# The closing Silu of each scan group, written as two ACT operations

## The chip, the cores and the metric

The kernel runs on one core of a Trainium2 chip. The metric is device time in microseconds (us) of one execution, 1267.39 us as the median of three runs (1267.34 to 1268.09). Times inside the kernel are read from one profiled execution, counted from the start of its span.

## What is computed

Two residual layers over 512 tokens of width 1024, each followed by a SwiGLU feed-forward part. Layer 0 mixes tokens in two ways at once: neighbourhood attention in 8 heads, and a bidirectional state-space scan (SSD) in 4 groups of 4 heads. The change sits in the scan's inputs:

```python
xbc = jax.nn.silu(centred_depthwise_conv(xbc, conv_w, conv_b))
xs, bm, cm = jnp.split(xbc, [...])
...
def gated_group_rms_norm(y, z, g):
    h = (y * jax.nn.silu(z)).astype(jnp.float32).reshape(Bsz, S, SSD_GROUPS, Dn // SSD_GROUPS)
    h = h * lax.rsqrt(jnp.mean(h * h, axis=-1, keepdims=True) + NORM_EPS)
    return (h.reshape(Bsz, S, Dn) * g.astype(jnp.float32)).astype(y.dtype)
```

So Silu is applied to x, B and C after a convolution of four taps, and to the gate z without one. The scan then takes exponentials of running sums; the norms take a reciprocal square root, made here as a logarithm (Ln), an exponential (Exp of -0.5 times it) and one Newton step.

## The kernel before, in words

Activations are kept transposed, 128 features by 512 tokens to a tile. Every product in full precision is three TensorE (PE) passes over two-part operands (`mm3`, lines 165 to 167); `load_w` (lines 145 to 161) fetches a weight tile by DMA, copies its high part on ScalarE (ACT, line 152, out `w_h` or `wo_h`, `wq_h`, `wf_h`) and subtracts on VectorE (DVE, line 154, out `w_l` and so on).

`even_mixer` is layer 0's mixer. Its PE work is one long stream, `fill`, of weight blocks of 24 matmuls (8 steps of 3), into which the attention's and the scan's own matmuls are put: `run(n)` takes n steps of `fill`. The blocks are query and key projections, then for each scan group g six blocks (`ssd_blocks`), then the output projection (`out_blocks`, PSUM tiles `oA` for what is ready early and `oB` for the last two groups, which are groups 2 and 3).

A group's six results make one tile `grp` (`gt` in the code) of 128 x 6 x 512. The blocks come in the order 4, 5, 0, 1, 2, 3. Parts 4 and 5 are z: a plain copy out of PSUM on ACT (line 546). Parts 0 to 3 are B, C and two tiles of x: `conv` makes one ACT operation (line 530) and three DVE operations (line 533) of each. After part 3 one Silu runs over the whole tile (line 550), and `preload_act_table_set(LNEXP)` (line 553) makes ACT load the table set that holds both Exp and Ln. `issue_after` puts that load behind the Silu, `high_priority` puts it there as early as may be. A load of a table set is an ACT instruction, ACT_TABLE_LOAD. Those that the code does not write are put by the compiler in front of an activation whose function is not in the set that is then loaded; for an Ln or an Exp alone it picks sets that do not hold the other one.

`ssd_group` scans a group: PE transposes B and x (`bt`, `xt`, lines 568 and 575), makes C times B (`cb`, line 581) and chunk states (`st`, line 604). For each half i of the heads (two heads, hh 0 and 1) ACT and DVE make the decay weights: ACT copies with scales (`m` line 640, `mb` 642), adds (`cf`, 643), takes an Exp (`cf<-cf`, line 650); DVE takes minima and multiplies (lines 645, 647, 649, 651). The product of line 651 is what PE's `yd` (line 656) needs, followed by `yo` (669) and DVE's sums into y (660 to 674). `ssd_norm` then makes the group's norm: squares (`gsq`, 686), `gs` on PE (693, 694), then on ACT `gn_m` (204), Ln (214), Exp (215), Square (216), Newton on DVE (208, 209), `yn` (698), and the two parts `so_xh` on ACT (188), `so_xl` on DVE (189), which the output projection reads. The norm's second piece is started NORM_LAG steps (12, 14, 10, 8) after its first; SSD_QUOTA gives the steps of `fill` between the pieces of a scan, LEAD (15, 12, 14, 8) those between a group's last block and its scan.

The feed-forward part of layer 0 begins with the same chain on one tile `fr` (`norm` in `ffn`, lines 1070 to 1073), whose result scales everything after it up to the hidden tiles (`hh`, `hl`), which the first matmuls of the down projection (`fo`) read.

The order of work: inside the scans PE's instructions stay as the program is written (`manual_schedule`); ACT, DVE, POOL and the DMA queue (SP) are ordered by a scheduler that takes what is ready by its own estimate, in the priority of program order. An instruction that becomes ready early may therefore be issued ahead of older ones. In the feed-forward part PE, DVE and ACT all stay as written. On the chip every engine runs its list strictly in order. Table loads that the compiler adds are put in after that ordering.

Of the kernel before, what the change touches and what calls it, by code (L numbers as in the profile page):

```python
# [11 lines left out]
AF = mybir.ActivationFunctionType  # L12
# [65 lines left out]
def encoder_kernel(ctx: ExitStack, tc: tile.TileContext, xt, vec, cst, rope, nab, w_v, w_qk, w_dt, w_ssd,  # L78
                   w_o0, w_t0, w_fa, w_fb, w_kv, w_gv, w_gq, w_o1, out):
    nc = tc.nc  # L80
    V, A, G, T = nc.vector, nc.scalar, nc.gpsimd, nc.tensor
# [13 lines left out]
    def bank(name, tag="p"):  # L95
        if tag in turns:
            turns[tag].append(turns[tag].pop(0))
            tag = turns[tag][-1]
        return pp.tile([P, S], F32, name=name, tag=f"p{tag}", bufs=BANKS[tag])
# [44 lines left out]
    def load_w(src, cols, name, eng=None, los=None):  # L144
        hi = wsp.tile([P, 1024], F32R, name=f"{name}_h", tag="wh", bufs=WH)
        lo = wsp.tile([P, 1024], F32R, name=f"{name}_l", tag="wl", bufs=WL)
        raw = wsp.tile([P, 1024], F32, name=f"{name}_r", tag="wr", bufs=WR)[:, 0:cols]
        parts = src if isinstance(src, list) else [src]
        for n, part in enumerate(parts):
            w = cols // len(parts)  # L150
            nc.sync.dma_start(raw[:, n * w:(n + 1) * w], part)
        A.activation(hi[:, 0:cols], raw, AF.Copy)  # L152
        def low():
            (eng or V).tensor_tensor(lo[:, 0:cols], raw, f(hi)[:, 0:cols], ALU.subtract)  # L154

        if los is None:
            low()
        else:
            los.append(low)
        return hi, lo  # L160

    def mm3(ps, w, wc, x, xc, first, last, wn=P, skip=False):
        (wh, wl), (xh, xl) = w, x
        a, b = slice(wc, wc + wn), xc
        T.matmul(ps, wl[:, a], xh[:, b], start=first, stop=False, skip_group_check=skip)  # L165
        T.matmul(ps, wh[:, a], xl[:, b], start=False, stop=False, skip_group_check=skip)  # L166
        T.matmul(ps, wh[:, a], xh[:, b], start=False, stop=last, skip_group_check=skip)  # L167
# [65 lines left out]
    def even_mixer(lp):  # L233
# [295 lines left out]
        def conv(ps, cb, o):  # L529
            A.activation(o, ps, AF.Identity, scale=vc("conv_w", cb * 4 + 2), bias=vc("conv_b", cb))  # L530
            for j in (0, 1, 3):
                a, b = max(0, 2 - j), min(S, S + 2 - j)
                V.scalar_tensor_tensor(o[:, a:b], ps[:, a + j - 2:b + j - 2], vc("conv_w", cb * 4 + j), o[:, a:b],
                                       ALU.mult, ALU.add)

        def ssd_blocks(g):
            gt = lp.tile([P, 6, S], F32, name=f"grp{g}", tag="grp", bufs=3)
            conv_cols = (8 + g, 12 + g, 2 * g, 2 * g + 1)

            def matmuls(w, i):  # L540
                ps = bank(f"g{g}_{i}")
                for k in range(KB):
                    mm3(ps, w, k * P, xn[k], ALL, k == 0, k == KB - 1)
                    yield
                if i > 3:
                    A.activation(gt[:, i], ps, AF.Copy)  # L546
                else:
                    conv(ps, conv_cols[i], gt[:, i])
                if i == 3:
                    si = A.activation(gt, gt, AF.Silu)  # L550
                    with tc.issue_after(si.ins):
                        with tc.high_priority():
                            A.preload_act_table_set(LNEXP)
                    ready[g] = gt

            for i in (4, 5, 0, 1, 2, 3):
                yield (lambda i=i: load_w(w_ssd[g * 6 + i], 1024, f"w{g}_{i}", V)), lambda w, i=i: matmuls(w, i)
# [1008 lines left out]
```

## Time and profile before

| | |
|---|---|
| median of 3 runs | 1267.39 us (1267.34 to 1268.09) |
| profiled execution, its own time | 1266.3 us |
| its span | 1264.5 us |
| granted TensorE clock, mean | 1.00 |
| the four scans and the end of layer 0's mixer | about 158 to 357 us |
| start of the feed-forward part of layer 0 | about 357 us |

A profile row of the timeline reads: start in us, duration in us, engine, line, operation, out<-in, shapes, number merged, and in brackets the idle time before it with what ended it. Neighbouring ACT operations overlap by about a tenth of a us, so a start-to-start distance is a little less than a duration. Rows of waits read: who waited, for whom, us in total, how often, longest.

### The profile page before, as it was taken

What the parts mean: (1) busy time and instruction counts of PE and PEld (TensorE: products, weight loads), DVE (VectorE), ACT (ScalarE), POOL (GpSimd) and SP (SyncE); (2) the same over time, 40 slices, a digit from 0 to 9 for tenths busy, and PEclk for the clock granted to TensorE, in tenths of its full rate; (3) what the DMA queues carried; (4) which work ended last, traced back from release to release, by engine and by line L of the source; (5) the groups of instructions that cost most, each with busy time, mean ns of one, the idle gap of its engine ahead of it and who ended that gap; (6) DMA issues with size and microseconds to landing.
All of it is one profiled execution on the core that took longest, in us unless ns stands there. A gap on an engine that the chain in (4) does not pass through costs nothing.

```text
span 1264.5 us, 20138 instructions
## 1 busy us (share of the span) xinstructions
PE 1252.1 (99%) x7574; PEld 1098.4 (87%) x7574; DVE 991.4 (78%) x1637; ACT 730.3 (58%) x1384; POOL 117.6 (9%) x161
## 2 busy tenths in 40 slices
PE   9999999999999999999999999999999999999998
PEld 8778788888788999989998888788888999889987
DVE  6788798999779988739854879998779988558732
ACT  6676578778464565415643558787554556336521
POOL 5022010011000000000000013444000000000000
PEclk9999999999999999999999999999999999999999
DMA  7335353556243333323223452321242333423132
GB/s 239 109 104 156 112 142 117 166 146 198 79 148 98 104 114 101 117 84 101 78 80 111 133 125 82 95 51 34 71 126 89 116 102 101 117 83 101 55 119 93
DMA packets 54241, 139.03 MB, mean 110 GB/s; under 512 B 7232, under 2 KB 9664, under 8 KB 54144
## 3 DMA queue, kind: packets, MB, share of 16 engines
q1 hardware_dynamic: 53712, 137.13, 35.8%
q8 instruction: 59, 0.97, 0.3%
q10 hardware_dynamic: 432, 0.63, 0.2%
q14 instruction: 38, 0.31, 0.1%
HBM read 127.11 MB, written 2.23 MB: 102 GB/s over the span
## 4 chain that ended last, share of the span: by engine, by line
PE 95%; ACT 2%; DVE 2%; issue 0%; DMA 0%; DVEq 0%; ACTq 0%
PE fo L166 6%; PE fo L167 6%; PE fo L165 6%; PE fa L167 5%; PE fa L166 5%; PE fa L165 5%; PE fu L1029 3%; PE fg L1029 3%; PE g L165 3%; PE g L166 3%; PE g L167 3%; PE fb L167 3%; PE fb L166 3%; PE fb L165 3%; PE opt L1311 2%; PE vps L286 2%
## 5 line engine op out<-in xcount | busy, mean ns | idle before, releaser
L165 PE MATMUL fo<-hh,wf_l 128*128 128x512 f32 x352 | 137.0, 389 | 0.0
L166 PE MATMUL fo<-hl,wf_h 128*128 128x512 f32 x352 | 137.0, 389 | 0.0
L167 PE MATMUL fo<-hh,wf_h 128*128 128x512 f32 x352 | 136.9, 389 | 0.0
L152 ACT ACTIVATE wf_h<-wf_r 128x1024 fp32r<-128x1024 f32 (+1 forms) x72 | 65.5, 913 | 119.2 <-PE fo L167 71.6
L1002 DVE TENSOR_TENSOR xr<-xr,fo 128x512 f32<-128x512 f32 (+1 forms) x49 | 32.1, 673 | 108.8 <-PE fo L167 108.8
L1302 POOL TENSOR_SCALAR op<-op,osum 128x512 f32<-128x512 f32 x64 | 45.6, 726 | 491.2 <-DMA QS<-qa_sh 433.5
L154 DVE TENSOR_TENSOR wf_l<-wf_r,wf_h 128x1024 fp32r<-128x1024 f32 (+1 forms) x72 | 74.0, 1044 | 11.0 <-ACT wf_h L152 11.0
L165 PEld LDWEIGHTS fo<-hh,wf_l 128*128 128x128 f32 x352 | 66.1, 188 | 13.7
L166 PEld LDWEIGHTS fo<-hl,wf_h 128*128 128x128 f32 x352 | 66.1, 188 | 13.7
L167 PEld LDWEIGHTS fo<-hh,wf_h 128*128 128x128 f32 x352 | 66.1, 188 | 13.6
L165 PE MATMUL g<-n_xh,w_l 128*128 128x512 f32 x192 | 76.9, 401 | 0.8 <-ACT grp L546 0.8
L166 PE MATMUL g<-n_xl,w_h 128*128 128x512 f32 x192 | 75.3, 392 | 0.5 <-DVE n_xl L189 0.5
L167 PE MATMUL g<-n_xh,w_h 128*128 128x512 f32 x192 | 75.3, 392 | 0.0
L926 ACT ACTIVATE sl<-sb 128x256 f32<-128x256 f32 x36 | 15.1, 419 | 96.1 <-DVE sb L925 96.1
L1298 ACT ACTIVATE op<-os,omx 128x512 f32<-128x512 f32 x64 | 43.8, 686 | 17.3 <-DVE omx L1296 13.5
L807 ACT ACTIVATE sa<-fa 128x256 f32<-128x256 f32 x72 | 26.9, 374 | 38.1 <-PE fa L167 38.1
L1296 DVE TENSOR_REDUCE omx<-os 128x1 f32<-128x512 f32 x64 | 42.5, 680 | 6.6 <-PE os L1294 6.5
L1315 DVE TENSOR_TENSOR opt<-opt,opt 128x512 fp32r<-128x512 f32 x64 | 43.3, 682 | 4.1 <-ACT opt L1314 3.3
L1314 ACT ACTIVATE opt<-opt 128x512 fp32r<-128x512 f32 x64 | 38.0, 596 | 14.0 <-PE opt L1311 13.3
L810 DVE TENSOR_TENSOR gl<-gr,gh 128x1024 fp32r<-128x1024 f32 x36 | 43.8, 1218 | 0.0
L165 PEld LDWEIGHTS g<-n_xh,w_l 128*128 128x128 f32 x192 | 36.1, 188 | 8.3 <-ACT grp L546 1.2
L807 ACT ACTIVATE gh<-gr 128x1024 fp32r<-128x1024 f32 x36 | 37.7, 1048 | 9.4 <-PE fo L167 9.4
(2745 smaller groups left out, 4305.4 us busy)
## 6 DMA issues: line engine op xcount, KB each, us to landing
ur<-in_w_fa SPq DMA_DIRECT2D x36, 512.0 KB, 3.6
gr<-in_w_fa SPq DMA_DIRECT2D x36, 512.0 KB, 3.6
w_r<-in_w_ssd SPq DMA_DIRECT2D x24, 512.0 KB, 3.6
wf_r<-in_w_fb SPq DMA_DIRECT2D x32, 320.0 KB, 3.0
wf_r<-in_w_fa SPq DMA_DIRECT2D x16, 512.0 KB, 3.6
wf_r<-in_w_fb SPq DMA_DIRECT2D x16, 512.0 KB, 3.5
nb<-in_nab SPq DMA_DIRECT2D x16, 256.0 KB, 3.2
ec<-ecumd SPq DMA_DIRECT2D x32, 128.0 KB, 3.0
```

The source lines that it names most:

```text
L152: A.activation(hi[:, 0:cols], raw, AF.Copy)
L154: (eng or V).tensor_tensor(lo[:, 0:cols], raw, f(hi)[:, 0:cols], ALU.subtract)
L165: T.matmul(ps, wl[:, a], xh[:, b], start=first, stop=False, skip_group_check=skip)
L166: T.matmul(ps, wh[:, a], xl[:, b], start=False, stop=False, skip_group_check=skip)
L167: T.matmul(ps, wh[:, a], xh[:, b], start=False, stop=last, skip_group_check=skip)
L807: A.activation(dst, src, AF.Copy, scale=scale)
L810: V.tensor_tensor(lo, t, f(hi), ALU.subtract)
L1029: T.matmul(ps, (wl if p == 0 else wh)[:, k * P:k * P + P], xl if p == 1 else xh, start=m == 0, stop=m == 23)
L1296: V.tensor_reduce(mx, sps, AX.X, ALU.max, negate=True)
L1298: A.activation(p_, sps, AF.Exp, bias=mx, accum_out=sums)
L1302: G.tensor_scalar(p_, p_, sums, 1.0, ALU.mult, ALU.mult)
L1315: V.tensor_tensor(hl[:, S:2 * S], pt, f(hl[:, 0:S]), ALU.subtract)
```

## The change

The Silu over six parts becomes two: parts 0 to 3 first, parts 4 and 5 second. The name `si`, behind which the load of the Exp and Ln set is put, now stands for the second.

```diff
                 if i == 3:
-                    si = A.activation(gt, gt, AF.Silu)
+                    A.activation(gt[:, 0:4], gt[:, 0:4], AF.Silu)
+                    si = A.activation(gt[:, 4:6], gt[:, 4:6], AF.Silu)
                     with tc.issue_after(si.ins):
                         with tc.high_priority():
                             A.preload_act_table_set(LNEXP)
```

The new operation on parts 4 and 5 reads nothing that the convolutions write. Lines behind it have a number higher by one in the changed kernel: its Silu of parts 4 and 5 is line 551, its written load of the set line 554, its Exp of the scan line 651.

The order of ACT's list in the two kernels, taken from the built programs, around the scan of group 2 (a load of a table is a row of its own there). In the kernel before, between the norm of group 1 and the Exp of the second head:

```order
L643 ACTIVATE cf_2895<-cf_2895,ncum 128x128 x4
L188 ACTIVATE so_0_xh<-yn_0_2689,vect 128x512
L530 ACTIVATE grp_393<-g_1_2714,vect 128x512
L188 ACTIVATE so_1_xh<-yn_1_2695,vect 128x512
L152 ACTIVATE wo_h<-wo_r 128x1024
L640 ACTIVATE m_2894<-cbl_2630,dt 128x128 x4
L650 ACTIVATE cf_2801<-cf_2801 128x512
```

The same place of ACT's list in the changed kernel:

```order
L644 ACTIVATE cf_2898<-cf_2898,ncum 128x128
L188 ACTIVATE so_0_xh<-yn_0_2692,vect 128x512
L530 ACTIVATE grp_393<-g_1_2717,vect 128x512
L188 ACTIVATE so_1_xh<-yn_1_2698,vect 128x512
L152 ACTIVATE wo_h<-wo_r 128x1024
L644 ACTIVATE cf_2898<-cf_2898,ncum 128x128 x3
L551 ACT_TABLE_LOAD
L551 ACTIVATE grp_393<-grp_393 128x1024
L554 ACT_TABLE_LOAD
L651 ACTIVATE cf_2804<-cf_2804 128x512
L530 ACTIVATE grp_393<-g_2_2773,vect 128x512
L641 ACTIVATE m_2897<-cbl_2633,dt 128x128 x4
```

The Silu of parts 4 and 5 of group 3 (`grp_393`), with a load on either side, now stands in front of the Exp of group 2's second head (`cf_2801` before, `cf_2804` now); four copies `m` moved behind that Exp. Groups 1 and 2 have their small Silu likewise in the scan of the group before, and group 0 in the attention.

ACT's list where the big Silu stands, group 2, in the kernel before:

```order
L550 ACT_TABLE_LOAD
L550 ACTIVATE grp_392<-grp_392 128x3072
L553 ACT_TABLE_LOAD
L686 ACTIVATE gsq_0_2580<-y_0_2404 128x512
L686 ACTIVATE gsq_1_2581<-y_1_2559 128x512
L152 ACTIVATE w_1_h<-w_1_r 128x1024
L689 ACTIVATE gs_qh<-gsq_0_2580 128x512
L650 ACTIVATE cf_2776<-cf_2776 128x512
L570 ACTIVATE btok_2609<-bt_2604 128x512
```

And now:

```order
L550 ACT_TABLE_LOAD
L550 ACTIVATE grp_392<-grp_392 128x2048
L152 ACTIVATE w_1_h<-w_1_r 128x1024
L687 ACTIVATE gsq_0_2583<-y_0_2406 128x512
L687 ACTIVATE gsq_1_2584<-y_1_2562 128x512
L651 ACT_TABLE_LOAD
L651 ACTIVATE cf_2779<-cf_2779 128x512
L690 ACTIVATE gs_qh<-gsq_0_2583 128x512
L546 ACTIVATE grp_393<-g_5_2550 128x512
L571 ACTIVATE btok_2612<-bt_2607 128x512
```

The written load of the common set went away with the small Silu; what follows the big one is a load that the compiler put in front of the first Exp, and the copy of the next group's part 5 moved ahead of `btok`.

The end of layer 0's mixer, ACT's norm of group 3, in the kernel before:

```order
L689 ACTIVATE gs_qh<-gsq_0_3450 128x512
L204 ACTIVATE gn_m<-gs_3495,epst 128x512
L214 ACTIVATE gn_r<-gn_m 128x512
L215 ACTIVATE gn_r<-gn_r 128x512
L216 ACTIVATE gn_t<-gn_r 128x512
```

And now:

```order
L690 ACTIVATE gs_qh<-gsq_0_3454 128x512
L204 ACTIVATE gn_m<-gs_3499,epst 128x512
L214 ACT_TABLE_LOAD
L214 ACTIVATE gn_r<-gn_m 128x512
L215 ACT_TABLE_LOAD
L215 ACTIVATE gn_r<-gn_r 128x512
L216 ACTIVATE gn_t<-gn_r 128x512
```

Ln and Exp of the chain each have a load of their own in front now. The norms of groups 0, 1 and 2 and the feed-forward norm `fr` of layer 0 show the same two loads; from the first Silu of that feed-forward part on, the lists of all engines are the same. In all, ACT's list held 12 table loads and holds 30.

## Prediction

> **What bounds the kernel now.** I read the page's first part and its chain first, then PE's waits over the part the change can touch, then the busy time there by stretch, then the rows at each place where PE takes something that ACT's list feeds.
>
> ```profile
> PE 1252.1 (99%) x7574; PEld 1098.4 (87%) x7574; DVE 991.4 (78%) x1637; ACT 730.3 (58%) x1384; POOL 117.6 (9%) x161
> PE 95%; ACT 2%; DVE 2%; issue 0%; DMA 0%; DVEq 0%; ACTq 0%
> ```
>
> PE is busy in all but 12.4 us of the span and carries the chain. PE's own work is not touched, so the most that could be won is a part of those 12.4 us, while anything that makes PE wait is added in full. The waits of PE between 140 and 420 us (total, times, longest):
>
> ```profile
> PE oA L165 <- ACT cf L643: 0.8, 1, 0.8
> PE g L165 <- ACT grp L546: 0.8, 1, 0.8
> PE bt L568 <- ACT grp L550: 0.5, 1, 0.5
> ```
>
> The big Silu (line 550) makes PE wait once, 0.5 us, at the last group's transposes. That is all that a shorter closing Silu can give back. How full the others are, in a stretch of the scans (columns: window, length, then busy us and instructions of PE, PEld, DVE, ACT, POOL):
>
> ```profile
> 260.00:300.00 40.00, 38.69 (x226) 32.37 (x225) 38.36 (x62) 31.23 (x61) 3.58 (x3) 1.00 0.50 140
> ```
>
> DVE is at 38.4 of 40 us, ACT at 31.2. The scan is a relay of ACT, DVE and PE with little spare, so the question is not ACT's average but where its added pieces stand.
>
> **What the change adds on ACT.** The Silu of group 0 and one that has 512 columns:
>
> ```profile
> 142.85 0.60 ACT L434 ACTIVATE nps<-npt 128x512 f32<-128x512 f32 x1 [0.30 <-PE npt L429]
> 143.47 1.28 ACT L550 ACT_TABLE_LOAD   x1
> 144.76 2.77 ACT L550 ACTIVATE grp<-grp 128x3072 f32<-128x3072 f32 x1
> 147.54 1.28 ACT L553 ACT_TABLE_LOAD   x1
> 372.69 0.64 ACT L1125 ACTIVATE s<-g 128x512 f32<-128x512 f32 x1 [0.98 <-DVE g L1124]
> ```
>
> A table load takes 1.28 us and blocks ACT. Silu costs (2.77 - 0.64) / 2560 = 0.83 ns a column, so 2048 columns are 1.92 us and 1024 are 1.07. The split itself adds 0.2 us a group. The order shows two other effects. The small Silu needs no convolution, so it now runs early, with a load on either side: a block of 1.28 + 1.07 + 1.28 = 3.63 us. And the written load of the common Ln and Exp set goes with it, so after the big Silu each Ln and each Exp that follows brings its own set: 30 loads for 12. The 18 new ones are 18 x 1.28 = 23.0 us of ACT time, and 23.9 with the splits. This is no loss by itself; what counts is what stands behind each.
>
> [...] The rows above show the 1.28 alone: the operation before the load ends at 143.45, the load begins at 143.47. [...]
>
> **The norm of group 3** (ACT, then DVE, then PE):
>
> ```profile
> 332.34 0.69 ACT L204 ACTIVATE gn_m<-gs,epst 128x512 f32<-128x512 f32 x1 [1.89 <-PE gs L694]
> 333.06 0.63 ACT L214 ACTIVATE gn_r<-gn_m 128x512 f32<-128x512 f32 x1
> 333.73 0.63 ACT L215 ACTIVATE gn_r<-gn_r 128x512 f32<-128x512 f32 x1
> 339.13 1.40 DVE L189 SCALAR_TENSOR_TENSOR so_xl<-yn,vect,so_xh 128x512 fp32r<-128x512 f32 x2
> 339.92 0.50 PE L166 MATMUL oB<-so_xl,wq_h 128*128 128x512 f32 x1
> ```
>
> The first `so_xl` is ready at about 339.83, PE takes it at 339.92: cover 0.1 us. Two loads, one before Ln and one before Exp, lie on this chain behind `gn_m`, which waits for PE: 2.57 - 0.1 = **2.5 us**.
>
> **The feed-forward norm**:
>
> ```profile
> 369.11 0.63 ACT L1072 ACTIVATE fr_r<-fr_r 128x512 f32<-128x512 f32 x1
> 370.42 1.28 ACT L1125 ACT_TABLE_LOAD   x1
> 409.00 0.69 DVE L810 TENSOR_TENSOR hl<-g,hh 128x512 fp32r<-128x512 f32 x1
> 409.91 0.39 PE L166 MATMUL fo<-hl,wf_h 128*128 128x512 f32 x1
> ```
>
> From the norm to the last hidden tile DVE works through its fixed list almost without a gap, and that tile is ready 0.2 us before PE reads it. The load in the second row, for Silu, is already hidden behind DVE's Newton step; the two new ones come before Ln and Exp and are not. 2.57 - 0.2 = **2.3 us**.
>
> **The scan of group 2**, first half (the Exp of the second head, its product on DVE, PE's `yd`):
>
> ```profile
> 248.58 0.60 ACT L546 ACTIVATE grp<-g 128x512 f32<-128x512 f32 x1
> 262.61 0.78 ACT L530 ACTIVATE grp<-g,vect 128x512 f32<-128x512 f32 x1 [0.21 <-PE g L167]
> 263.91 1.05 ACT L152 ACTIVATE wo_h<-wo_r 128x1024 fp32r<-128x1024 f32 x1
> 266.14 1.28 ACT L640 ACTIVATE m<-cbl,dt 128x128 f32<-128x128 f32 x4 [1.19 <-DVE m L647]
> 267.40 0.63 ACT L650 ACTIVATE cf<-cf 128x512 f32<-128x512 f32 x1
> 269.01 0.69 DVE L651 TENSOR_TENSOR cf<-cf,m 128x512 f32<-128x512 f32 x1
> 269.98 1.09 PE L656 MATMUL yd<-cf,xtok 128*64 128x128 f32 x16
> ```
>
> The product ends at 269.70 and PE starts 0.28 later. In the new list the copy of part 5 (248.58, held by PE's block) stands before `btok` and the `xtok` copies, which puts these and what follows about 1.1 us later. The norm of group 1 brings two loads, 2.57. The 0.2 us wait at 262.61 and about 0.1 more are absorbed. So `wo_h` ends at 264.9 + 3.4 = 268.3, the small Silu's block 3.63 later at 271.9; the four `m` with their wait no longer stand in front. Exp ends at 272.5, the product at 273.1, against 269.98: **3.1 us** of waiting at `yd`. Queued behind this on DVE are the convolution of part 2 and the weight of the next block, but PE stands too, so both lose about the same.
>
> **The scan of group 1**:
>
> ```profile
> 215.28 0.72 ACT L188 ACTIVATE so_xh<-yn,vect 128x512 fp32r<-128x512 f32 x1 [0.40 <-DVE yn L698]
> 221.13 0.62 ACT L650 ACTIVATE cf<-cf 128x512 f32<-128x512 f32 x1
> 222.67 0.67 DVE L651 TENSOR_TENSOR cf<-cf,m 128x512 f32<-128x512 f32 x1
> 223.70 1.09 PE L656 MATMUL yd<-cf,xtok 128*64 128x128 f32 x16
> ```
>
> Here the two loads before the norm of group 0 lose about 1.0 to the wait on `yn` and to copies `m` and `mb` done sooner, leaving 1.6. The small block adds 3.63; a convolution copy, a weight copy and two `m` (0.68 + 0.95 + 0.6 = 2.2 by the rows above) have moved behind the Exp. It starts 3.0 later, at 224.1, ends at 224.7; the product ends at 225.4, and with the hand-over PE's `yd` stands **1.8 us**.
>
> **The scan of group 3** (no small Silu is left to insert, but two loads of group 2's norm are):
>
> ```profile
> 299.62 0.64 ACT L216 ACTIVATE gn_t<-gn_r 128x512 f32<-128x512 f32 x1
> 310.30 0.68 DVE L651 TENSOR_TENSOR cf<-cf,m 128x512 f32<-128x512 f32 x1
> 311.54 1.09 PE L656 MATMUL yd<-cf,xtok 128*64 128x128 f32 x16
> ```
>
> The big Silu is 0.85 shorter, so the 0.5 us wait at `bt` goes; late next is this: the list now has `gn_m` soon after the transposes, and DVE's list the Newton step ahead of both heads' products. `gn_t` ends 1.6 us later (two loads, part of it won by the early place), at 301.9; DVE then needs the 10.0 us that lie between `gn_t` and the product's end before, and one piece of 0.7 more: 312.6 against 311.54. Net of the 0.5, which is in it: **1.2 us**.
>
> **The attention**, where group 0's Silu pair stands. A load now stands before the last head's Exp, and it waits for the same DVE result as the Exp did:
>
> ```profile
> 150.22 1.92 POOL L419 TENSOR_SCALAR ns<-ns,nsum 128x256 f32<-128x256 f32 x4 [22.80 <-DVE nsum L416]
> 153.09 1.03 PE L429 MATMUL npt<-cstt,ns 128*128 128x128 f32 x8
> ```
>
> POOL ends at 152.14, 0.95 us before PE; the Exp comes about 1.5 later, and PE's list now has these transposes earlier. I take **0.6 us**, between 0 and 1.5. The scan of group 0 itself has LEAD 15 and I charge nothing to it; at zero cover it would cost up to 2.
>
> **The sum.** 0.6 + 1.8 + 3.1 + 1.2 + 2.5 + 2.3 = 11.5 us; stalls add, since each shifts all that follows. The profiled execution's own time is 1266.3 (span 1264.5), so it would become 1277.8. That execution lies 1.1 under the median of the runs, so the median becomes 1267.39 + 11.5 = **1278.9 us**.
>
> **The rivals.** A measurement can tell about 0.2% (2.5 us) of this kernel from no change.
>
> *Only the fixed lists pay* (chance 0.14): in the scans the scheduler's new order keeps the relay as full as before, since what moved behind the Exp pays for the block. For it: ACT has nearly 9 idle us in the 40 above. Against it: cover of only 0.3 us at `yd`. Then 2.5 + 2.3 remain, and 1272.2 us.
>
> *The load passes through* (0.12): DVE, which has 1.6 us free in 40, cannot make up what it loses waiting, so lateness of one half becomes lateness of the next, and convolutions and weights come late too. The end is all of ACT's new time, 23.9: 1291.3; a likelier case is that nothing of the loads is absorbed, 1.5 in the attention, 2.57 + 3.63 - 2.2 - 0.4 = 3.6 in group 1, 2.57 + 1.1 + 3.63 - 2.4 - 0.3 = 4.6 in group 2, 2.6 in group 3, and 2.5 + 2.4 behind them: 17.2, or 1284.6.
>
> *A load holds ACT twice as long* (0.02), a stop of about its own length before it: the terms grow by 5.1 for each four loads in groups 1 and 2, 2.6 for each two in group 3 and in the two late norms: 18.0 more, 1296.9. Against it is the row at 143.47. [...]
>
> *Not slower* (0.04): the loads run in ACT's waits. The place is the norm of group 3: ACT idles 1.89 us before `gn_m`, and a load of 1.28 issued in that wait would cost nothing. It decides from a cover of 2.6 us at the two late norms and at `yd`; then only the 0.5 at `bt` is left: 1266.9. Against it, the list puts the load behind `gn_m`, and Exp's behind Ln.
>
> **How the numbers follow.** My forecast has 0.68, of which the larger part lies between 1274 and 1283. Below, the norms' loads in the scans are wholly absorbed: 0 in the attention, 3.63 - 2.2 - 0.4 = 1.0 in group 1, of which the 0.9 between Exp and product may also go, 3.63 - 2.4 - 0.3 = 0.9 in group 2, a gain of 0.5 in group 3, and 2.4 + 2.1 behind: 5.0 us, or 1272.4. Above stand the 17.2. The first rival lies at 1272.2, so the range is 1272.0 to 1284.6, which leaves out the rest of the second rival, the third and the fourth. Faster by over 0.2%: 0.02. Within it: 0.03. Slower: 0.95.
>
> **What would show it.** In the changed profile: 30 loads of 1.28; PE waiting on the Exp's product at `yd` in groups 1, 2 and 3; about 2.5 us at `oB` on `so_xl` and 2.3 at `fo` on `hl`; the wait at `bt` gone; PE's busy time unchanged. It is wrong if the waits at `oB` and `fo` are under 1 us, or if `yd` does not wait.

## The result and the profile after

The changed kernel takes 1284.72 us (median of 4 executions, 1283.65 to 1285.66); the kernel before took 1267.47 us beside it (1267.34 to 1268.09). The ratio is 1.0135, 95% interval 1.0117 to 1.0152: 17.25 us slower. The prediction was 1278.9 us, 1272.0 to 1284.6. So the direction came out, the amount is 5.8 us above the number and 0.1 us above the upper end, which is less than the spread of the executions.

The profiled execution took 1285.49 us (span 1283.7). First the page's busy times, the shares of its chain, and its row of the granted clock in 40 slices:

```profile
PE 1261.4 (98%) x7574; PEld 1103.4 (86%) x7574; DVE 991.4 (77%) x1637; ACT 754.7 (59%) x1406; POOL 118.5 (9%) x161
PE 86%; ACT 7%; DVE 5%; issue 2%; DMA 0%; DVEq 0%; ACTq 0%
PEclk9999999989999999999999999999999999999999
```

ACT has 24.4 us more, close to the 23.9 that 18 loads and four splits make. ACT and DVE now hold 12% of the chain, where they held 4. Two things stand here that the prediction did not have: PE's own busy time is 9.3 us longer although its work is the same, and one slice of the clock, the ninth, is below full. PE's waits between 140 and 440 us:

```profile
PE yd L657 <- DVE cf L652: 6.1, 3, 3.3
PE fo L165 <- ACT hh L808: 1.4, 1, 1.4
PE oB L165 <- DVE xr L712: 1.3, 1, 1.3
PE st L605 <- DVE xw L593: 1.0, 1, 1.0
PE oB L166 <- DVE so_xl L189: 0.8, 1, 0.8
...
PE fo L166 <- DVE hl L811: 0.2, 1, 0.2
```

Summed waits do not say where the time went, because an earlier wait can swallow a later one. For that, one takes matmuls that both traces have and looks at how their distance grows (the starts in both are from the timelines, the differences are worked out):

| matmul | before | after | after - before | added here | predicted |
|---|---|---|---|---|---|
| `nsc`, attention | 57.54 | 58.69 | 1.15 | | |
| `xt`, group 0 | 158.91 | 160.34 | 1.43 | 0.3 | 0.6 |
| `g`, late in the scan of group 1 | 238.01 | 242.42 | 4.41 | 3.0 | 1.8 |
| `bt`, group 3 | 286.96 | 297.14 | 10.18 | 5.8 | 3.1 |
| `yo`, group 3, first half | 312.57 | 326.82 | 14.25 | 4.1 | 1.2 |
| `oB` on `so_xl` | 339.92 | 356.75 | 16.83 | 2.6 | 2.5 |
| `fo`, six matmuls behind the first on the last hidden tile | 411.29 | 430.38 | 19.09 | 2.3 | 2.3 |

The first 1.15 us stand ahead of all that the change touches, and with them 1.2 of PE's 9.3 us. Behind the last row nothing is added. The 0.5 us wait at `bt` that went is in group 2's row here and in group 3's in the prediction. The six places make 17.9 us where 11.5 was forecast: the two late norms as predicted, the scans 6.8 too little.

**Half clock.** PE's rows at the first `yd` of groups 1 and 2:

```profile
227.44 1.09 PE L657 MATMUL yd<-cf,xtok 128*64 128x128 f32 x14 [1.89 <-DVE cf L652]
278.00 1.97 PE L657 MATMUL yd<-cf,xtok 128*64 128x128 f32 x14 [3.28 <-DVE cf L652]
279.90 2.93 PE L670 MATMUL yo<-grp,H 128*128 128x128 f32 x12
```

And windows at the two waits (window, length, busy us and count of PE, PEld, DVE, ACT, POOL, then the granted clock):

```profile
229.20:232.60 3.40, 3.40 (x13) 3.01 (x13) 3.40 (x6) 3.40 (x13) 1.05 (x1) 0.52 0.60 184
276.80:280.20 3.40, 2.20 (x15) 1.87 (x16) 2.53 (x5) 3.40 (x8) 0.56 (x1) 0.50 0.67 211
280.20:283.60 3.40, 3.40 (x15) 3.21 (x15) 2.51 (x5) 2.27 (x8) 1.54 (x2) 0.50 0.34 102
```

Windows of 0.1 us place the edges:

```profile
229.00:229.10 0.10, 0.10 (x3) 0.10 (x2) 0.10 (x1) 0.10 (x1) 0.00 (x0) 0.62 0.76 225
232.40:232.50 0.10, 0.10 (x2) 0.09 (x1) 0.10 (x1) 0.10 (x1) 0.00 (x0) 0.81 0.99 410
276.80:276.90 0.10, 0.00 (x0) 0.00 (x0) 0.00 (x0) 0.10 (x1) 0.00 (x0) 0.56 0.00 0
283.60:283.70 0.10, 0.10 (x2) 0.10 (x1) 0.10 (x1) 0.00 (x0) 0.00 (x0) 0.80 0.00 0
```

In group 1 the granted clock is 0.50 from 229.02 to 232.44 us (3.4 us, beginning 1.6 behind the end of the wait), in group 2 from 276.81 to 283.64 (6.8 us, beginning 1.2 before the end of the wait). The `yd` that took 1.09 takes 1.97, and twelve `yo` 2.93 instead of 1.60. Compared start to start, PE lost 1.6 us to that in group 1 and 2.6 in group 2: 4.2 us with no wait to show for them.

**What stands ahead of the late product.** ACT's rows in the scan of group 2 (the norm of group 1, then the small Silu):

```profile
258.10 0.69 ACT L204 ACTIVATE gn_m<-gs,epst 128x512 f32<-128x512 f32 x1
...
259.58 1.28 ACT L214 ACT_TABLE_LOAD   x1
260.87 0.63 ACT L214 ACTIVATE gn_r<-gn_m 128x512 f32<-128x512 f32 x1
261.41 1.04 ACT L152 ACTIVATE w_h<-w_r 128x1024 fp32r<-128x1024 f32 x1
262.47 1.28 ACT L215 ACT_TABLE_LOAD   x1
...
264.78 0.62 ACT L216 ACTIVATE gn_t<-gn_r 128x512 f32<-128x512 f32 x1
...
272.93 1.28 ACT L551 ACT_TABLE_LOAD   x1
274.22 1.06 ACT L551 ACTIVATE grp<-grp 128x1024 f32<-128x1024 f32 x1
275.30 1.28 ACT L554 ACT_TABLE_LOAD   x1
```

And the places where DVE stands in the same stretch, its brackets being what to read:

```profile
262.48 1.23 DVE L154 TENSOR_TENSOR w_l<-w_r,w_h 128x1024 fp32r<-128x1024 f32 x1 [0.88 <-ACT w_h L152]
265.43 0.69 DVE L208 SCALAR_TENSOR_TENSOR gn_t<-gn_t,gn_m 128x512 f32<-128x512 f32 x1 [1.72 <-ACT gn_t L216]
277.25 0.69 DVE L652 TENSOR_TENSOR cf<-cf,m 128x512 f32<-128x512 f32 x1 [0.47 <-ACT cf L651]
```

There are two candidates, and both are in the prediction: the loads of the norm (DVE stands 0.88 and 1.72 us at what is behind them) and the block around the small Silu, right in front of the Exp. The last bracket bounds the second: from 265.43 on DVE works through its list almost without a gap, and it stands only 0.47 us for the Exp. So with the same list and no block the product could have come 0.47 us earlier at most. Group 1 shows the same on DVE, after a longer stop for a copy (`H`) that ACT makes behind the norm's second load:

```profile
214.63 0.69 DVE L611 TENSOR_TENSOR H<-H,dec 128x512 f32<-128x512 f32 x1 [3.21 <-ACT H L609]
...
226.69 0.69 DVE L652 TENSOR_TENSOR cf<-cf,m 128x512 f32<-128x512 f32 x1 [0.48 <-ACT cf L651]
```

These brackets point at the norm's loads. They hold for the order that the lists have here, and say nothing of the times that another order would give. Over most of the scans of groups 1 to 3 the sums of the windows from 206 to 330 us, of before and of after, show whose time was lost:

```profile
sum 124.00, PE 121.92 PEld 102.08 DVE 116.01 ACT 94.13 POOL 15.07; mean PE 24.39 PEld 20.42 DVE 23.20 ACT 18.83 POOL 3.01
```

```profile
sum 124.00, PE 115.74 PEld 95.90 DVE 104.33 ACT 103.99 POOL 15.35; mean PE 23.15 PEld 19.18 DVE 20.87 ACT 20.80 POOL 3.07
```

DVE went from 8.0 to 19.7 us of idle time in 124. It is the engine with the least to spare after PE.

### The profile page after: what moved, and what is told of

The parts are those of the page before. It is cut to its first block, busy times and chain, and to the rows that moved or that the text cites. A ratio compares the mean times of both kernels' runs of the same rounds, so it can differ in the third digit from the quotient of the medians.

```text
span 1283.7 us, 20165 instructions
## 1 busy us (share of the span) xinstructions
PE 1261.4 (98%) x7574; PEld 1103.4 (86%) x7574; DVE 991.4 (77%) x1637; ACT 754.7 (59%) x1406; POOL 118.5 (9%) x161
## 4 chain that ended last, share of the span: by engine, by line
PE 86%; ACT 7%; DVE 5%; issue 2%; DMA 0%; DVEq 0%; ACTq 0%
PE fo L166 6%; PE fo L167 6%; PE fo L165 6%; PE fa L167 5%; PE fa L166 5%; PE fa L165 5%; PE fb L167 3%; PE fb L166 3%; PE fb L165 3%; PE fg L1030 3%; PE g L165 2%; PE g L167 2%; PE g L166 2%; PE fu L1030 2%; PE opt L1312 2%; PE vps L286 2%
## 5 line engine op out<-in xcount | busy, mean ns | idle before, releaser
L167 PEld LDWEIGHTS g<-n_xh,w_h 128*128 128x128 f32 x192 | 36.4, 189 | 7.7 <-issue 0.2
```

## The experiments

Theory 1: the loss comes from where the loads stand. The early small Silu and the loads of the norms both pay at places with little cover, and waits of PE bring half clock on top. Theory 2: the loss goes with ACT's added time, or with the split itself, wherever it stands.

**The split alone, in order** (the change, with this edit). The small Silu and then the set are tied behind the big one:

```diff
-                    A.activation(gt[:, 0:4], gt[:, 0:4], AF.Silu)
-                    si = A.activation(gt[:, 4:6], gt[:, 4:6], AF.Silu)
+                    first = A.activation(gt[:, 0:4], gt[:, 0:4], AF.Silu)
+                    with tc.issue_after(first.ins):
+                        with tc.high_priority():
+                            si = A.activation(gt[:, 4:6], gt[:, 4:6], AF.Silu)
```

> The Silu is still made in two operations, but the second is tied right behind the first on ACT and the common Ln and Exp set behind the second, so the list has 12 table loads again and nothing of the Silu runs early. Theory 1 (the loss comes from where the loads stand, not from the split): ACT busy 730.3 + 4 x 0.2 = 731.1 us, granted clock 1.00 throughout, no wait at yd; 1267.4 us, from 1266.8 (the 0.5 us wait at bt goes, since the transposes need only the first operation) to 1268.2 (the 0.2 us a group shows). Theory 2 (two operations cost by themselves, as a semaphore or a second start on the path): 1270 us or more, up to the 1284.7 of the change.

Measured: 1269.4 us, ratio 1.0013 (1.0005 to 1.0022), with 12 loads. With the split in this order the kernel takes 1.75 us more (0.6 to 2.8 by the interval), not 17. That is more than theory 1 allowed (1268.2) and less than theory 2 asked for (1270 or more). In the trace the order in the scan of group 2 came out a little differently, and one wait of 2.3 us stands there, of which 0.9 is handed back further on.

```profile
PE yd L659 <- DVE cf L654: 2.3, 1, 2.3
```

**The early small Silu alone** (again the change). Only the set is tied to the other operation:

```diff
-                    A.activation(gt[:, 0:4], gt[:, 0:4], AF.Silu)
-                    si = A.activation(gt[:, 4:6], gt[:, 4:6], AF.Silu)
+                    si = A.activation(gt[:, 0:4], gt[:, 0:4], AF.Silu)
+                    A.activation(gt[:, 4:6], gt[:, 4:6], AF.Silu)
```

> The split stays, and so does the early small Silu with a load on either side; the common set is tied to the big Silu, so that no Ln or Exp of a norm brings a load: 20 loads, 10 fewer than in the change. Theory 1 (each place pays its own loads, less its cover): the 2.5 us at oB and 2.2 us at fo go, so do the 4.1 us of group 3; at yd the small block alone is left, 1.89 - 1.6 = 0.3 us in group 1 and 3.28 - 2.3 = 1.0 us in group 2, too short for the half clock; 1267.5 + 0.3 + 0.3 + 1.0 = 1269.1 us (1268 to 1271.5). Theory 2 (the loss goes with ACT's added time, wherever it stands): 8 new loads and the splits are 11.1 of the 24.4 us, 0.455 x 17.25 = 7.8 us, 1275.3 us.

Measured: 1267.44 us, ratio 1.0 (0.9991 to 1.0009). Eight more loads than before, four early Silus, and no loss that can be told (the interval leaves 1.1 us either way). Theory 2 with its 1275.3 falls, and theory 1 asked too much as well: 1269.1, from 1268 to 1271.5. ACT's rows in the scan of group 1 show that the block really stands in front of the Exp:

```profile
219.50 1.28 ACT L551 ACT_TABLE_LOAD   x1
220.80 1.06 ACT L551 ACTIVATE grp<-grp 128x1024 f32<-128x1024 f32 x1
221.88 1.28 ACT L651 ACT_TABLE_LOAD   x1
223.17 0.63 ACT L651 ACTIVATE cf<-cf 128x512 f32<-128x512 f32 x1
```

PE's rows at the first `yd` of groups 1 and 2 show what comes of it:

```profile
224.58 1.09 PE L657 MATMUL yd<-cf,xtok 128*64 128x128 f32 x14 [0.16 <-DVE cf L652]
...
271.44 1.09 PE L657 MATMUL yd<-cf,xtok 128*64 128x128 f32 x14 [1.19 <-DVE cf L652]
```

The Exp of group 1 is 2.0 us later than before (223.17 against 221.13), but PE waits 0.2 us in all; in group 2 it is 1.2. And both are given back: the distance to the kernel before falls by 0.9 us at each of two later waits, `g` on the copy of part 4 and `oA`, which took 0.8 us before and are gone here. So what the prediction took for about half of the loss in groups 1 and 2 costs nothing while the norms bring no loads.

**The missing set alone.** The kernel before with one Silu, and without the written load:

```diff
-                    si = A.activation(gt, gt, AF.Silu)
-                    with tc.issue_after(si.ins):
-                        with tc.high_priority():
-                            A.preload_act_table_set(LNEXP)
+                    A.activation(gt, gt, AF.Silu)
```

> The kernel before with its one Silu in its old place, and only the written load of the common set left out, so that each Ln and Exp of a norm and the first Exp of a scan bring their own: 22 loads, none in front of the second head's Exp at yd. Theory 1: the 2.5 us at oB and 2.2 us at fo come as in the change; in the scans of groups 1 to 3 two loads stand behind gn_m, which is 2.57 less an absorbed 1.0 to 2.3, so 0.3 to 1.6 us each, 1 to 4.8 together, and the clock stays at 1.00 if no single wait is near 1.9 us; 1267.5 + 4.7 + 3 = 1275 us (1273 to 1277). Theory 2 (by ACT's added time, 10 x 1.28 = 12.8 of 24.4 us): 9.0 us, 1276.5 us, but spread over the scans and with under 2 us at oB and fo together.

Measured: 1283.87 us, ratio 1.0125 (1.0111 to 1.0139): 16.2 of the change's 17.25 us, without any split and without an early Silu. Theory 1's amount (1275) fails like theory 2's. PE's late waits are those of the change (`fo` 1.5 us, `oB` 1.3 and 0.8), and `yd` is worse:

```profile
PE yd L653 <- DVE cf L648: 7.7, 3, 4.3
PE bt L565 <- DVE yd L670: 1.8, 1, 1.8
```

So theory 1 has to be narrowed to the loads that this run has: those at a scan's first Exp and those at the norms' Ln and Exp. The next runs ask whether they pay place by place.

**Group 2 alone, group 3 alone.** The written load is left out in one group (the edit for group 2; for group 3 it reads `if g != 3`):

```diff
                     si = A.activation(gt, gt, AF.Silu)
-                    with tc.issue_after(si.ins):
-                        with tc.high_priority():
-                            A.preload_act_table_set(LNEXP)
+                    if g != 2:
+                        with tc.issue_after(si.ins):
+                            with tc.high_priority():
+                                A.preload_act_table_set(LNEXP)
```

> The kernel before, one Silu in its old place, and the written load of the common set left out in group 2 alone: 14 loads, of which two stand at the Ln and the Exp of group 1's norm in the middle of group 2's scan. Theory 1 (the norm's loads make gn_t and the copy H late, DVE's in-order list stands behind them, and the lost DVE time comes out at yd): DVE waits for gn_t and for conv and weight copies, 3 to 4 us more than before, PE waits about 4.3 us at yd as in the run without any written set, about 2.0 us of half clock follow and 0.9 us is handed back: 1267.6 + 5.4 = 1273.0 us (1270.5 to 1274). Theory 2 (loss by ACT's added time, 17.25 us for 24.4): 2.57 us give 1.8, 1269.4 us.

> The same with the written load left out in group 3 alone: 18 loads, the added ones at the first Exp and at the norm of group 2 inside group 3's scan, at the norm of group 3 and at the feed-forward norm. Theory 1: 2.6 to 3.8 us in the scan (st and yd together), 2.6 at oB, 2.1 at fo, the half clock only if one of these waits happens to bring it (1.8 us at fo in the run without any written set): 1267.6 + 8 = 1275.6 us (1274.5 to 1277.5). With group 2 alone this adds up to nearly all of the 16.2 us of that run; groups 0 and 1 are left with 1 to 2. Theory 2 (by ACT's added time): 6 x 1.28 = 7.7 us give 5.4, 1273.0 us.

Measured: 1273.34 us (ratio 1.0045, 1.003 to 1.006) and 1275.28 us (1.007, 1.0053 to 1.0087), beside 1266.99 for the kernel before. Both fall where theory 1 put them, theory 2's 1269.4 and 1273.0 do not. Together they are 6.35 + 8.29 = 14.6 of the 16.2 us. DVE's rows in group 2 that begin with a stop:

```profile
250.03 2.50 DVE L593 TENSOR_TENSOR xw<-xtok,wst 128x512 f32<-128x512 f32 x4 [1.02 <-ACT xtok L578]
254.27 0.84 DVE L648 TENSOR_TENSOR m<-m,mb 128x512 f32<-128x512 f32 x1 [0.61 <-ACT mb L643]
257.94 1.53 DVE L533 SCALAR_TENSOR_TENSOR grp<-g,vect,grp 128x510 f32<-128x510 f32 x2 [2.10 <-ACT grp L530]
260.89 0.69 DVE L208 SCALAR_TENSOR_TENSOR gn_t<-gn_t,gn_m 128x512 f32<-128x512 f32 x1 [1.41 <-ACT gn_t L216]
```

At the last two DVE stands 3.5 us in its fixed list: at a convolution whose copy on ACT is queued behind Ln's load, and at the Newton step, which needs what comes behind Exp's. The first two, 1.6 us, are for copies that stand behind another load, the one in front of the scan's first Exp, which now comes at 247.09 us and no longer right behind the Silu. They lie ahead of the convolution, for which DVE stands anyway, so they may be taken up there; no run separates this load from the norm's. In the stretch from 250 to 274 us before, DVE had one such wait:

```profile
255.29 1.53 DVE L533 SCALAR_TENSOR_TENSOR grp<-g,vect,grp 128x510 f32<-128x510 f32 x2 [1.28 <-ACT grp L530]
```

The loss then appears at three places of PE, `w_l` 1.2, `yd` 2.2 and `bt` 1.8, none of them on the norm itself. So the amount came as expected, but not its place: 4.3 us had been expected at `yd` alone.

**One load at the norm instead of two**: the kernel that leaves the set out in group 2, with the set written once behind `gn_m` of that norm:

```diff
-        A.activation(m, ps, AF.Identity, scale=inv, bias=epst)
+        mi = A.activation(m, ps, AF.Identity, scale=inv, bias=epst)
+        if name == "gn1":
+            with tc.issue_after(mi.ins):
+                with tc.high_priority():
+                    A.preload_act_table_set(LNEXP)
```

> The kernel without the written set in group 2, but with that set loaded once behind gn_m of group 1's norm, so that Ln and Exp share it: 13 loads, one of 1.28 us in front of gn_t where the run before had two. Theory 1 (DVE's in-order list stands behind gn_t): gn_t comes 1.3 us earlier, DVE's waits for gn_t and the conv copy behind the load shrink by about 1.3 us each at most, and a part of the loss remains, since DVE has about 1.4 us free in 24 there: from 1273.3 back to about 1269.5 us (1268 to 1271), with no half clock if no wait of PE is over 1.5 us. Rival (each load passes in full, 1.28 us of 6.3): 1272.0 us. Second rival (the loss is that of the missing early set at the first Exp, not of the norm): 1273.3 us.

Measured: 1270.11 us, ratio 1.0023 (1.0014 to 1.0033), 2.7 us over its kernel before. One load of 1.28 us at this place is worth 6.35 - 2.66 = 3.7 us. That is within what theory 1 gave and under both rivals (1272.0 if the load is passed on in full, 1273.3 if the loss is that of the first Exp). How the 3.7 divide, the half clock explains in part (below). The 2.7 us that remain belong to the other load at the norm and to that at the first Exp together.

**Keeping PE busy.** The change, with matmuls that nothing reads in PE's list in front of `yd`:

```diff
                 yield 2 + 2 * i
+                if i == 0:
+                    for _ in range((0, 4, 7, 0)[g]):
+                        T.matmul(yd, bT[:, 0:P], cT, start=True, stop=True)
```

> The change, with matmuls that nothing reads put on PE in front of the first yd: 4 in group 1 and 7 in group 2, 128x512 with operands that are long there, about 0.45 us each by the yo rows (1.60 us for twelve of 128 columns), into the bank that yd then overwrites. They leave ACT's and DVE's work as it is and only keep PE busy where it stood 1.9 and 3.3 us. Theory 1 (the half clock comes from PE standing): the granted clock stays at 1.00 through both groups, yd starts no later, and the 1.7 + 2.8 us of half clock go: 1284.7 - 4.5 = 1280.2 us. Rival (the half clock has another cause, or the filler only adds itself): 1284.7 us, up to 1289.7 with 11 x 0.45 us on the path.

Measured: 1289.11 us, ratio 1.0173 (1.0158 to 1.0189). Theory 1's 1280.2 did not come, and the time lies at the rival's upper end. But the run does not settle the matter: such a matmul runs as two of 0.45 us, so the filler was twice as long as meant, and the scheduler reordered ACT's list from group 2 on. What it shows is group 1, where four of them filled the wait and the clock stayed up:

```profile
224.39 3.60 PE L657 MATMUL yd<-grp 128*128 128x512 f32 x8
```

```profile
229.20:232.60 3.40, 3.40 (x22) 3.02 (x22) 3.40 (x6) 3.31 (x9) 1.05 (x1) 1.00 0.71 211
```

Again with the right length, on the kernel that leaves the set out in group 2 (the same lines with `if g == 2 and i == 0`, and 3 or 4 of them):

> The kernel without the written set in group 2, with 3 matmuls that nothing reads in front of group 2's first yd (0.90 us each, as the filler of the earlier run measured), 2.7 us of PE work in a wait of about 4.3 us. Theory 1 (the half clock follows from PE standing): the wait listed at yd falls to about 1.6 us, yd itself starts no later, the clock stays at 1.00, and the time falls by the 2.0 us of half clock, 1271.0 us. Rival (the clock does not depend on it): half clock as without filler, 1273.0 us; if the filler only adds itself, 1275.7 us.

> The same with 4 such matmuls, 3.6 us of PE work in the same wait. Theory 1: about 0.7 us of waiting left at yd, the clock at 1.00, 1271.0 us. Rival: 1273.0 us, or 1276.6 us if the filler only adds itself.

Measured: 1274.75 us (ratio 1.0055, 1.004 to 1.007) and 1271.86 us (1.0036, 1.0023 to 1.0049), beside 1273.34 without filler. With three, theory 1's 1271.0 did not come. With four the time lies near it, but the interval also holds the rival's 1273.0, so the clock has to decide. With four the clock stays at 1.00 through the place where it was 0.84 and 0.66 without; the windows of the kernel without filler, then of that with four:

```profile
273.40:276.80 3.40, 2.23 (x20) 2.06 (x21) 3.36 (x6) 2.47 (x7) 1.05 (x1) 0.84 0.71 201
276.80:280.20 3.40, 3.40 (x15) 3.03 (x15) 2.28 (x5) 0.92 (x4) 1.05 (x1) 0.66 0.26 96
```

```profile
273.40:276.80 3.40, 3.40 (x15) 1.45 (x16) 3.40 (x6) 2.48 (x6) 0.00 (x0) 1.00 0.49 119
276.80:280.20 3.40, 3.40 (x31) 2.97 (x28) 3.40 (x8) 2.48 (x8) 2.14 (x1) 1.00 0.80 263
```

The lists differ in other places too: at `bt` of group 3 PE waits 1.3 us with four and 1.8 without. With three, the executions at a mean granted clock of 0.999 took 1274.56 to 1275.22 us and the one at 1.000 took 1272.46; where the clock fell in them is not shown. The single executions agree without any filler. Without the set in group 2 the four took 1273.42, 1273.89 and 1273.25 us at a mean granted clock of 0.999, 0.998 and 0.999, and 1271.60 at 1.000. With one load at the norm, eight executions at 1.000 took 1269.62 to 1270.57, two at 0.999 took 1271.55 and 1271.63. So either kernel is some 1.5 to 2 us longer in executions with the lower clock. Only one execution of each has a trace, and a mean of 0.999 alone is no mark: in the run with the set tied to the big Silu the fastest executions have 0.999 and 1.000 alike (1267.12 and 1267.09).

**Five parts early**, a version that might beat both (the kernel before, with this edit):

```diff
+                if i == 2:
+                    A.activation(gt[:, 0:3], gt[:, 0:3], AF.Silu)
+                    si = A.activation(gt[:, 4:6], gt[:, 4:6], AF.Silu)
+                    with tc.issue_after(si.ins):
+                        with tc.high_priority():
+                            A.preload_act_table_set(LNEXP)
                 if i == 3:
-                    si = A.activation(gt, gt, AF.Silu)
+                    si = A.activation(gt[:, 3], gt[:, 3], AF.Silu)
```

> A version that might beat both: parts 0 to 2 and 4 to 5 of each group in two operations ahead of the last convolution, part 3 alone at the end, and the common set written behind each, so that no norm brings a load; 26 loads. Theory 1 (a load costs only where DVE's list waits for what stands behind it): the closing Silu is 0.64 us where it was 2.77, so the waits for it (0.5 to 0.9 us at bt, 0.8 at the copy of part 4) go and up to 1.3 us is won, 1266.3 us; against it the loads of part 3 stand near the first Exp of the next scan, which may cost 0 to 3 us: 1267.5 us (1266 to 1270). Rival (loss by ACT's added time, 14 loads and the splits, 19 us): 13 us, 1280 us.

> The version with five parts early once more, with more executions, since its interval (0.9983 to 1.0002) did not tell it from the kernel before. Theory 1 (waits for the closing Silu, 0.5 at bt and 0.8 at the copy of part 4, are won and nothing else is lost): 1266.4 us, ratio 0.9992. Rival (no difference): 1267.4 us, ratio 1.0.

Measured: 1266.38 us against 1267.45 (ratio 0.9992, 0.9983 to 1.0002), and again 1265.8 against 1267.26 (0.9991, 0.9982 to 1.0). The gain is about 1 us, at the edge of what can be told. For the question it is a clear run. The sum over the same 124 us:

```profile
sum 124.00, PE 122.85 PEld 103.28 DVE 117.72 ACT 105.81 POOL 15.51; mean PE 40.95 PEld 34.43 DVE 39.24 ACT 35.27 POOL 5.17
```

ACT is busier here than in the change (105.81 against 103.99) and has 26 loads in all, and DVE idles 6.3 us, less than in the kernel before. So the number of loads does not decide. That it matters whether one stands in front of something that DVE's list waits for fits this run and those before it.

## Why the prediction was right and where it was wrong

- **Direction, loads and ACT's time: right.** 30 loads, 24.4 us more on ACT (23.9 forecast), and the written set drawn away from the big Silu as the cause of the loads at the norms.
- **The late norms: right in size.** 2.6 us at `oB` and 2.3 at `fo`, for 2.5 and 2.3; the run with group 3 alone has the same waits. At `oB` the way was another in part: of the two waits the first, 1.30 us, is on `xr`, the addition that hands back a PSUM bank and stands in DVE's list behind the late Newton step; only 0.84 is on `so_xl`.
- **The attention: right**, 0.3 us for 0.6.
- **The scan of group 1 and of group 2: waits nearly as forecast (1.89 and 3.28 for 1.8 and 3.1), for the wrong reason.** That they came so near is luck. The failing step is the sum in which the small Silu's block of 3.63 us stands in front of the Exp and comes out at `yd` less what moved behind it. Alone it makes PE wait 0.2 and 1.2 us and costs nothing in the end, and in the change itself DVE stands only 0.48 and 0.47 us for the Exp behind it. Without any early Silu, the loads at the first Exp and at the norm bring a wait of 4.3 us in group 2 where no set is written, and taking away one load at the norm gave 3.7 us back. The forecast let these loads pass through ACT only, to the next Exp; they pass through DVE, which is nearly full (38.4 of 40 us) and takes its list in order: its 1637 instructions in the profile of the change stand in the order of the program's list, as ACT's 1280 activations do.
- **"Stalls add, since each shifts all that follows": wrong for the first 0.9 us of a group.** A wait of 0.8 us that follows anyway takes an earlier one up, 0.9 us start to start.
- **The scan of group 3: too small, 4.1 us for 1.2.** The wait at `bt` went as forecast. But the `st` matmuls wait 0.98 for `xw` and are stretched from 2.84 to 4.08 us, and DVE stands 3.39 us at the Newton step, where the forecast allowed 1.6 for the late `gn_t`. (Its 10.0 us from `gn_t` to the end of the product reach only to the product's start at 310.30. So the 0.7 that it adds is the product itself, and its sum has no room for one more piece.) PE's rows, then DVE's:

```profile
308.14 4.08 PE L605 MATMUL st<-xw,btok 128*128 128x128 f32 x24 [0.98 <-DVE xw L593]
...
325.80 1.09 PE L657 MATMUL yd<-cf,xtok 128*64 128x128 f32 x14 [0.94 <-DVE cf L652]
```

```profile
313.28 1.21 DVE L208 SCALAR_TENSOR_TENSOR gn_t<-gn_t,gn_m 128x512 f32<-128x512 f32 x1 [3.39 <-ACT gn_t L216]
```

- **"PE's busy time unchanged": wrong.** The half clock around the waits at `yd`, 1.6 + 2.6 us, was no term of the sum. It (4.2 us) and group 3 (2.9 us) cover the 6.4 us between 11.5 and 17.9.
- **The rivals.** "The load passes through" was the nearest (1284.6 in its likelier case), and its mechanism, DVE with 1.6 us to spare in 40, is the one the runs bear out, though it starts at the norm and not at the small Silu. That its total fits so well is luck too: its terms are 1.2 us too high in the attention, 1.2 and 1.5 too low in the scans of groups 2 and 3, and none is the half clock. "Only the fixed lists pay" falls with the 12.9 us of the scans, "not slower" with the result; a norm's load in a wait of ACT was not what came. The stop ahead of a load, by which a load would hold ACT twice as long, is shown by no run: in the rows of the run with the early small Silu alone the next operation starts 1.3 us after a load does, and the load at 221.88 starts 0.02 us after the operation ahead of it ends.

Left open: how much the early Silu adds when the norms do bring loads. The brackets allow about 0.5 us in each of groups 1 and 2 with the lists as they are; what its reordering of the lists does is not in them. The change and the run without any written set differ by 0.85 us, which is inside their spread, and the second has a half clock at `fo` (1.8 us) that the first has not.

## What to carry to other kernels

When a change ties a written table load to an operation that becomes ready early, look at which later activations lose their set: here these loads, not those around the moved operation, were the price. Price an ACT delay by the next in-order engine that waits for it: beside a full DVE, one load of 1.28 us cost 3.7 us with the half clock that followed, while eight around the early Silus cost nothing where the norms had none. To place a loss, compare the starts of the same matmuls in both traces, since listed waits leave out a lower clock and waits that take one another up.

## What the runs showed of the hardware

In the change the granted clock fell to 0.50 around two waits of PE: for 3.4 us around one of 1.89, for 6.8 us around one of 3.28. The shortest with which it fell in a profile were 1.47 and 0.22 us close together at `fo` in the run without any written set, and PE's rows and a window show the step:

```profile
424.77 0.50 PE L165 MATMUL fo<-hh,wf_l 128*128 128x512 f32 x1 [1.47 <-ACT hh L804]
425.49 0.50 PE L166 MATMUL fo<-hl,wf_h 128*128 128x512 f32 x1 [0.22 <-DVE hl L807]
...
426.57 0.63 PE L167 MATMUL fo<-hh,wf_h 128*128 128x512 f32 x1
```

```profile
426.40:429.80 3.40, 3.40 (x10) 2.63 (x9) 2.98 (x6) 1.06 (x1) 0.00 (x0) 0.51 0.00 0
```

The same wait in the change (1.45 and 0.23 us) did not bring it (1.00 from 419.60 to 433.20 us), nor did it in the run with group 3 alone (mean granted clock 1.0 in its profiled execution), nor did one of 2.55 us in the filled kernel (1.00 from 250.00 to 296.00). So the length of a wait alone does not decide; what else does is not shown.
